# Moving the norm-weight products and the sums of the early banks in the last pass of a GeGLU down projection

## The chip, the cores and the metric

The kernel runs on one core of a Trainium2 chip. A core has five engines with queues of their own: TensorE (PE in the profile, with its weight loads as PEld), VectorE (DVE), ScalarE (ACT), GpSimd (POOL) and SyncE (SP, which here issues nearly all DMA transfers). Each engine works through its queue in order; an instruction that waits for a semaphore holds up everything behind it. The metric is the device time of one execution in microseconds, as the median of three runs.

## The reference, cut to what matters

One decoder layer over 256 tokens of 2048 numbers, in float32. The change touches only its last lines:

```
u = causal_dwconv(h @ w_up[l], conv_w[l], conv_b[l])
gate, val = jnp.split(u, 2, axis=-1)
y = (jax.nn.gelu(gate, approximate=True) * val) @ w_down[l]     # 256 x 5632 @ 5632 x 2048
x = x + rmsnorm(y, post_ffn_g[l])     # y * rsqrt(mean(y*y) + eps) * post_ffn_g
```

A token's row of y must be complete before its reciprocal root (rsqrt of the mean square over all 2048 columns) is known. The product of y with `post_ffn_g` needs no such row and can be made earlier.

## The kernel before, in words

Tokens are in two tiles of 128 (t = 0, 1), the 2048 output columns in four blocks of 512 (n = 0 to 3). The down projection runs in two halves of the 5632 inner rows, and each half in two passes over the columns, n = 0 with 1 and n = 2 with 3. So there are four passes, and the last is half 1, columns 1024 to 2047. Each pass reads 22 blocks of 128 rows of `w_down`, in 11 units of two blocks, each block 128x1024 (512 KB).

A float32 product is made of three passes of a faster format (`product`, line 964): high times high, high times low and low times high. For that each weight block is split: ScalarE copies it rounded (`split`, line 312, the high part `whi`), and VectorE subtracts that from the original (line 313, the low part `wlo`). A low part of 128x1024 is one VectorE instruction. TensorE cannot do the second of three matmuls before it.

Four units of a pass (`FAST`) go by a scheme of seven products in place of eight, with sums of weight quarters (lines 1007 to 1013, VectorE) and of activations. Their first four products gather in the early banks m1, m5, m7, m6 (PSUM tag acc), the others in the late banks p2, p3, p4, p22 (tag att), where the other units gather too. After the last `FAST` unit `add_early` adds the early banks to y in SBUF: one ScalarE copy of m1 into `s`, and eight VectorE sums of 128x512. In the last pass, `HOLD` = 3 units are held back: their parts are made and kept, and `block(i)` runs their 18 matmuls for one late bank after the other, so that one block of y is complete while the next still runs. This is the kept part. The last of the three units has its parts in a tile `rest`. Block 3 is made in two pieces of 256 columns.

`down(t, n, ...)` (line 1087) completes a block of y: VectorE adds the bank (line 1090), ScalarE squares with a row sum (line 1091), GpSimd multiplies by the norm's weights `gbf` (line 1092, called "the product" below). It runs for columns n = 0 and 1 at the end of the third pass, and for n = 2 and 3 in the kept part. `before_last` and `rstd_y` (lines 1160 to 1172) make the reciprocal root: two small VectorE instructions, after the last square one more (line 1169), then a GpSimd power (line 1171). `finish` (line 1175) is one VectorE instruction per block, y times the root plus the residual `x_back`, and the store of the block.

Before the kept part a planner sets the order of each engine but TensorE, whose order is the written one. In the kept part the written order holds for all of them.

Of the kernel before, what the change touches and what calls it, by code (L numbers as in the profile page):

```python
# [12 lines left out]
ALU = mybir.AluOpType  # L13
# [18 lines left out]
def hybrid_layer(ctx: ExitStack, tc: tile.TileContext, x, pre_mix_g, w_in, b_forget, sinks,  # L32
# [814 lines left out]
    with tc.tile_pool(name="ffn", bufs=1) as fp:  # L847
# [122 lines left out]
        def fast_pass(G, sums, order, k00, c0, load, tb, early, late, add_early, hold=1,  # L970
                      keep=None):

            left, right = slice(0, 512), slice(512, UNIT)
            fast = [u for u in order if u in FAST]

            def of(k, t):
                return G[k][:, t * P:(t + 1) * P], G[k][:, 256 + t * P:256 + (t + 1) * P]

            def parts(src, n, into=None):
                hi, lo = into or w_parts(n)  # L980
                split(hi, lo, src)
# [12 lines left out]
            for u in order:  # L994
                k = 2 * u
                ra, rb = (load(w_rows(w_down, k00 + k + a, 1, c0, UNIT)) for a in range(2))
                if u in FAST:
                    i = FAST.index(u)
                    end = u == fast[-1]

                    def s_of(j):
                        return (sums[:, i, j * P:(j + 1) * P],
                                sums[:, i, 512 + j * P:512 + (j + 1) * P])

                    b11 = parts(ra[:, left], 512)
# [12 lines left out]
                    product(m5, *s_of(0), f13, left, first(m5), end)  # L1018
                    product(m7, *s_of(2), f13, right, first(m7), end)
                    product(m6, *s_of(1), f24, left, first(m6), end)  # L1020
                    product(p4, *of(k + 1, 1), f24, right, first(p4), False)
                    product(p2, *of(k + 1, 0), b2, left, first(p2), False)
                    product(p3, *s_of(3), b2, right, first(p3), False)
                    if end:
                        add_early()
                    continue
                b = [parts(r, UNIT, keep[a] if keep and u == order[-1] else None)
                     for a, r in enumerate((ra, rb))]
                if u in order[-hold:]:
                    held += [(k + a, b[a]) for a in range(2)]  # L1030
                    continue
                for a in range(2):
                    for bk, t, cols in blocks:
                        product(bk, *of(k + a, t), b[a], cols, first(bk),
                                hold > 1 and bk is p22 and u == order[-hold - 1] and a == 1)

            def block(i, bk=None, cols=None):
                b, t, c = blocks[i]
                for n, (k, w) in enumerate(held):
                    product(bk or b, *of(k, t), w, cols or c, bk is not None and n == 0,  # L1040
                            n == len(held) - 1, cols and slice(cols.start - 512, cols.stop - 512))

            return block
# [3 lines left out]
        for half in range(2):  # L1047
# [31 lines left out]
                        sums = main.tile([P, len(FAST), UNIT], F32R, tag="x", name="sums")  # L1079
                    token_sums(sums[:, FAST.index(g), :], *ys)  # L1080
            if half == 1:
                late_room = main.tile([P, 4 * D], F32, tag="hT", name="late_room")
                gbf = late_room[:, 0:D]
                x_back = late_room[:, D:3 * D].rearrange("p (t c) -> p t c", t=2)
                sp.dma_start(gbf, post_ffn_g[0].partition_broadcast(P))

            def down(t, n, b, h=None, into=None):
                i, cs = (n, slice(0, 512)) if h is None else (n + h, slice(h * 256, h * 256 + 256))
                ys = y_sb[:, t, n * 512:(n + 1) * 512][:, cs]
                dve.tensor_tensor(ys, b[:, cs], ys, op=ALU.add)  # L1090
                act.activation(junk[:, cs], ys, AF.Square, accum_out=ysq[t][:, i:i + 1])
                pool.tensor_tensor(ys if into is None else into, ys,
                                   gbf[:, n * 512:(n + 1) * 512][:, cs], op=ALU.mult)

            extra = fp.tile([P, 2, UNIT], F32, tag="gbc", name="extra")
            tb = fp.tile([P, 3, UNIT], F32, tag="room", name="tb")
# [11 lines left out]
            for n in (0, 2):  # L1108
                early, late = ([bank(tag) for _ in range(4)] for tag in ("acc", "att"))
                order = list(range(FHALF // 2))  # L1110
                if n == 0:
                    order[:9] = [1, 3, 0, 5, 2, 7, 4, 8, 6]
                elif half:
                    for t in range(2):
                        sp.dma_start(x_back[:, t, :], x_dram[t * P:(t + 1) * P, :])

                def y_of(t, c):
                    return y_sb[:, t, (n + c) * 512:(n + c + 1) * 512]
# [54 lines left out]

        def finish(t, cs, r, q, y=None):
            dve.scalar_tensor_tensor(y_sb[:, t, cs], y_sb[:, t, cs] if y is None else y, r,
                                     x_back[:, t, cs], op0=ALU.mult, op1=ALU.add)
            q.dma_start(of[t * P:(t + 1) * P, cs], y_sb[:, t, cs])

        ctx.enter_context(tc.manual_schedule(
            engines={mybir.EngineType.Activation, mybir.EngineType.DVE, mybir.EngineType.Pool,  # L1180
                     mybir.EngineType.SP}))
        block(0)
        down(0, 2, late[0])
        v = before_last(0, 3)
        block(1)
        down(0, 3, late[1])
        r = rstd_y(0, 3, v)
        for n in range(4):
            finish(0, slice(n * 512, (n + 1) * 512), r, sp)
        block(2)  # L1190
        down(1, 2, late[2])
        last = fp.tile([P, 256], F32, tag="last", name="last")
        for h in range(2):
            if h:
                v = before_last(1, 4)
            b = bank()
            block(3, b, slice(512 + h * 256, 768 + h * 256))
            down(1, 3, b, h, last if h else None)
        r = rstd_y(1, 4, v)
        for i, n in enumerate((512, 512, 512, 256, 256)):  # L1200
            c = (0, 512, 1024, 1536, 1792)[i]
            finish(1, slice(c, c + n), r, (sp, act)[i % 2], last if i == 4 else None)
# [29 lines left out]
```

## Time and profile before

| | |
|---|---|
| median of 3 runs | 1070.96 us (1070.40 to 1071.10) |
| the profiled execution's own time | 1070.95 us |
| its span, first to last instruction | 1069.2 us |
| TensorE busy | 1052.4 us (98%), granted clock 0.997 |
| VectorE, ScalarE, GpSimd busy | 843.4, 637.2, 224.8 us |
| third pass of `down` ends, last pass starts | about 998 us |
| kept part starts, TensorE's last matmul ends | about 1042 us, 1060.2 us |

Times in what follows are microseconds from the span's start. In a timeline a row gives the start, the length, the engine, the line, the operation, the tiles, the count of equal instructions that follow each other, and in brackets the idle time before it with what ended it. Instructions of one engine overlap a little: the next one starts some 0.08 us before the former ends.

### The profile page before, as it was taken

How to read it: one execution, taken by the hardware profiler on the slowest of the kernel's cores; microseconds unless marked ns; L12 is line 12 of the kernel's file. 1: busy time of each engine (PE TensorE's matmuls, PEld its weight loads, DVE VectorE, ACT ScalarE, POOL GpSimd, SP SyncE). 2: the span in 40 equal slices, each digit the busy share in tenths (PEclk: the TensorE clock that was granted, in tenths of full speed). 3: DMA queues.
4: the chain of work that ended last, by engine and by line, in shares of the span. 5: the costliest groups of instructions: out<-in, count | busy, mean ns of one | idle time of the engine just before them, and what ended most of it. 6: DMA issues, size and time to landing. Idle time of an engine off the chain costs nothing.

```text
span 1069.2 us, 16290 instructions
## 1 busy us (share of the span) xinstructions
PE 1052.4 (98%) x5890; PEld 912.9 (85%) x5890; DVE 843.4 (79%) x1369; ACT 637.2 (60%) x1096; POOL 224.8 (21%) x256
## 2 busy tenths in 40 slices
PE   9999999999999999999999999999999999999996
PEld 7889988887889988888888888888888888888785
DVE  5988877887567887787767989668777787788995
ACT  7766766666556765565655556446555565656561
POOL 3233343342022121221212000002121211200202
PEclk9999999999999999999999999999999999999998
DMA  8645657555873776665666566666566666685552
GB/s 291 206 120 174 180 160 210 161 153 156 300 248 106 266 229 188 192 190 181 211 186 191 192 203 209 215 187 197 167 209 190 190 191 195 192 301 191 167 175 79
DMA packets 154284, 207.08 MB, mean 194 GB/s; under 512 B 6844, under 2 KB 131036, under 8 KB 153180
## 3 DMA queue, kind: packets, MB, share of 16 engines
q1 hardware_dynamic: 153200, 203.37, 60.5%
q10 hardware_dynamic: 1004, 2.68, 0.6%
q8 instruction: 46, 0.75, 0.3%
q14 instruction: 34, 0.28, 0.1%
HBM read 201.68 MB, written 4.21 MB: 193 GB/s over the span
## 4 chain that ended last, share of the span: by engine, by line
PE 90%; DVE 4%; DMA 2%; issue 2%; POOL 1%; ACT 1%; SPq 0%; DVEq 0%; POOLq 0%; ACTq 0%
PE bank_acc L284 16%; PE bank_att L967 14%; PE bank_att L284 14%; PE bank_acc L309 12%; PE bank_acc L290 8%; PE bank_att L290 7%; PE bank_acc L253 6%; PE bank_acc L967 4%; PE bank_acc L258 3%; PE bank_att L475 1%; DVE wlo L313 1%; PE bank_att L510 1%; DVE wlo L115 1%; PE bank_acc L932 1%; DMA x_in<-in_x_dram 1%
## 5 line engine op out<-in xcount | busy, mean ns | idle before, releaser
L115 DVE TENSOR_TENSOR wlo<-raw,whi 128x1024 fp32r<-128x1024 f32 (+3 forms) x271 | 330.1, 1228 | 117.1 <-ACT whi L112 112.4
L112 ACT CAST whi<-raw 128x1024 fp32r<-128x1024 f32 (+3 forms) x270 | 273.3, 1029 | 124.4 <-issue 88.9
L899 POOL TENSOR_TENSOR room<-room,rowf 128x256 f32<-128x256 f32 x88 | 100.3, 1160 | 393.9 <-DVE room L898 392.1
L284 PE MATMUL bank_acc<-hT,whi 128*128 128x512 f32 x736 | 173.3, 390 | 0.0
L284 PEld LDWEIGHTS bank_acc<-hT,whi 128*128 128x128 f32 x736 | 136.5, 188 | 27.3
L967 PE MATMUL bank_att<-whi,G 128*128 128x512 f32 x488 | 156.2, 389 | 0.0
L284 PE MATMUL bank_att<-hT,whi 128*128 128x512 f32 x640 | 150.6, 390 | 0.0
L284 PEld LDWEIGHTS bank_att<-hT,whi 128*128 128x128 f32 x640 | 118.7, 188 | 23.8
L967 PEld LDWEIGHTS bank_att<-whi,G 128*128 128x128 f32 x488 | 91.6, 188 | 18.9
L967 PE MATMUL bank_att<-wlo,G 128*128 128x512 f32 x244 | 95.2, 390 | 2.4 <-DVE wlo L313 2.4
L290 PEld LDWEIGHTS bank_acc<-hT,wlo 128*128 128x128 f32 x736 | 89.3, 188 | 2.0
L290 PE MATMUL bank_acc<-hT,wlo 128*128 128x256 f32 x736 | 89.9, 279 | 0.0
L253 PE MATMUL bank_acc<-hT,whi 128*128 128x512 f32 x352 | 89.2, 396 | 0.0
L901 ACT ACTIVATE room<-room,cw 128x256 f32<-128x256 f32 x88 | 53.0, 602 | 60.6 <-POOL room L899 60.6
L309 PE MATMUL bank_acc<-whi,oT 128*128 128x512 f32 (+1 forms) x272 | 82.5, 380 | 0.0
L290 PEld LDWEIGHTS bank_att<-hT,wlo 128*128 128x128 f32 x640 | 77.6, 188 | 1.7
L290 PE MATMUL bank_att<-hT,wlo 128*128 128x256 f32 x640 | 77.9, 279 | 0.0
L903 DVE SCALAR_TENSOR_TENSOR room<-room,cw 128x256 f32<-128x256 f32 x88 | 62.4, 709 | 17.5 <-ACT room L901 17.3
L313 DVE TENSOR_TENSOR wlo<-raw,whi 128x1024 fp32r<-128x1024 f32 (+1 forms) x56 | 62.4, 1138 | 13.4 <-ACT whi L312 13.4
L253 PEld LDWEIGHTS bank_acc<-hT,whi 128*128 128x128 f32 x352 | 63.0, 188 | 11.3
L312 ACT CAST whi<-tb 128x1024 fp32r<-128x1024 f32 x42 | 44.0, 1050 | 45.0 <-PE bank_att L967 19.2
L312 ACT CAST whi<-raw 128x1024 fp32r<-128x1024 f32 (+1 forms) x56 | 52.4, 958 | 28.8 <-PE bank_att L967 22.2
(254 smaller groups left out, 1589.9 us busy)
## 6 DMA issues: line engine op xcount, KB each, us to landing
raw<-in_w_up_dram SPq DMA_DIRECT2D x176, 512.0 KB, 4.1
raw<-in_w_down_dram SPq DMA_DIRECT2D x58, 512.0 KB, 4.8
raw<-in_w_in_dram SPq DMA_DIRECT2D x51, 512.0 KB, 3.9
raw<-in_w_out_dram SPq DMA_DIRECT2D x32, 512.0 KB, 4.7
extra<-in_w_down_dram SPq DMA_DIRECT2D x20, 512.0 KB, 3.8
raw<-in_w_in_dram SPq DMA_DIRECT2D x16, 384.0 KB, 3.4
tb<-in_w_down_dram SPq DMA_DIRECT2D x10, 512.0 KB, 4.8
cb<-c_dram SPq DMA_DIRECT2D x8, 256.0 KB, 3.6
```

Source lines behind the costliest of these rows:

```text
L112: i1 = act.copy(hi[:, cs], raw[:, cs])
L115: i2 = dve.tensor_tensor(lo[:, cs], raw[:, cs], hi[:, cs].bitcast(F32), op=ALU.subtract)
L253: pe.matmul(b, parts[u][0][:, a, m * P:(m + 1) * P], hT[:, kt, :], start=(kt == 0), stop=(kt == KT - 1))
L284: pe.matmul(b, parts[u][0][:, a, m * P:(m + 1) * P], hT[:, kt, :], start=(kt == 0), stop=(kt == KT - 1))
L290: pe.matmul(b[:, 256:512], parts[u][1][:, a, m * P:(m + 1) * P], hT[:, kt, 0:256], start=False, stop=False)
L309: pe.matmul(b, a, r[:, cols], start=(first and i == 0), stop=(last and i == 2))
L312: act.copy(hi, src)
L313: dve.tensor_tensor(lo, src, hi.bitcast(F32), op=ALU.subtract)
L899: pool.tensor_tensor(u[:, 2:258], u[:, 2:258], rowf, op=ALU.mult)
L901: act.activation(y, u[:, 2:258], AF.Identity, bias=cw[:, 3, ch:ch + 1], scale=cw[:, 2, ch:ch + 1])
L903: dve.scalar_tensor_tensor(y, u[:, 1:257], cw[:, 1, ch:ch + 1], y, op0=ALU.mult, op1=ALU.add)
L967: pe.matmul(b[:, to] if to else b, a, r[:, cols], start=(first and i == 0), stop=(last and i == 2))
```

## The change

1. `down` makes no product any more. The products of all blocks are made by a new function `gain`, called in the kept part.
2. In the last pass `add_early` is called after the loop over the units (`if hold > 1`), no longer inside it. In the other passes it stays.
3. The residual `x_back` is no longer loaded into its own room at the third pass's start, but into two buffers, `tb[:, 0:2]` and `extra`, that served as room for sums and weights, at the start of the kept part as written.
4. Two of the four `finish` of token tile 0 come after the sum of block (1, 2).
5. In the tail the power for token tile 1 comes ahead of the last product.

```
-                    if end:
+                    if end and hold == 1:
                         add_early()
...
+            if hold > 1:
+                add_early()
...
-                late_room = main.tile([P, 4 * D], F32, tag="hT", name="late_room")
-                gbf = late_room[:, 0:D]
-                x_back = late_room[:, D:3 * D].rearrange("p (t c) -> p t c", t=2)
+                gbf = main.tile([P, 4 * D], F32, tag="hT", name="gbc_ffn")[:, 0:D]
...
+            def gain(t, n, h=None, into=None):
+                cs = slice(0, 512) if h is None else slice(h * 256, h * 256 + 256)
+                ys = y_sb[:, t, n * 512:(n + 1) * 512][:, cs]
+                pool.tensor_tensor(ys if into is None else into, ys,
+                                   gbf[:, n * 512:(n + 1) * 512][:, cs], op=ALU.mult)
...
-                pool.tensor_tensor(ys if into is None else into, ys,
-                                   gbf[:, n * 512:(n + 1) * 512][:, cs], op=ALU.mult)
...
-                elif half:
-                    for t in range(2):
-                        sp.dma_start(x_back[:, t, :], x_dram[t * P:(t + 1) * P, :])
...
+        x_back = [tb[:, 0:2, :].rearrange("p a c -> p (a c)"),
+                  extra.rearrange("p a c -> p (a c)")]
+        for t in range(2):
+            sp.dma_start(x_back[t], x_dram[t * P:(t + 1) * P, :])
+        gain(0, 0)
+        gain(0, 1)
         block(0)
         down(0, 2, late[0])
+        gain(0, 2)
+        gain(1, 0)
         v = before_last(0, 3)
         block(1)
         down(0, 3, late[1])
         r = rstd_y(0, 3, v)
-        for n in range(4):
+        gain(0, 3)
+        gain(1, 1)
+        for n in range(2):
             finish(0, slice(n * 512, (n + 1) * 512), r, sp)
         block(2)
         down(1, 2, late[2])
+        gain(1, 2)
+        for n in range(2, 4):
+            finish(0, slice(n * 512, (n + 1) * 512), r, sp)
...
-            down(1, 3, b, h, last if h else None)
+            down(1, 3, b, h)
+            if h == 0:
+                gain(1, 3, 0)
         r = rstd_y(1, 4, v)
+        gain(1, 3, 1, last)
```

GpSimd, all that it has to do after the up projection. Before, the eight products stand in the order of `down` (0,0), (0,1), (1,0), (1,1), (0,2), (0,3), and behind the first power (`ry`) (1,2) and the two halves of (1,3):

```order
L1092 TENSOR_TENSOR y_sb<-y_sb,late_room 128x512 x6
L1171 TENSOR_TENSOR ry<-rv,mhalf 128x1
L1092 TENSOR_TENSOR y_sb<-y_sb,late_room 128x512
L1092 TENSOR_TENSOR y_sb<-y_sb,late_room 128x256
L1092 TENSOR_TENSOR last<-y_sb,late_room 128x256
L1171 TENSOR_TENSOR ry<-rv,mhalf 128x1
```

Changed, the first four are (0,0), (0,1), (0,2), (1,0), and the three behind the first power (0,3), (1,1), (1,2):

```order
L1091 TENSOR_TENSOR y_sb<-y_sb,gbc_ffn 128x512 x4
L1173 TENSOR_TENSOR ry<-rv,mhalf 128x1
L1091 TENSOR_TENSOR y_sb<-y_sb,gbc_ffn 128x512 x3
L1091 TENSOR_TENSOR y_sb<-y_sb,gbc_ffn 128x256
L1173 TENSOR_TENSOR ry<-rv,mhalf 128x1
L1091 TENSOR_TENSOR last<-y_sb,gbc_ffn 128x256
```

The products (0,0) and (0,1) are still the first in GpSimd's queue behind the up projection's work, and each waits for the square of its own block alone; (1,0) and (1,1) now stand behind instructions that wait for blocks of the kept part; the second power stands ahead of the last product.

VectorE in the last pass, from the low part of the unit behind the last `FAST` one (before; `s` and `y_sb` in the outputs are `add_early`, `wlo` and `rest` low parts):

```order
L1131 TENSOR_TENSOR y_sb<-s,y_sb 128x512
L313 TENSOR_TENSOR wlo<-extra,whi 128x1024
L1132 TENSOR_TENSOR s<-bank_acc,s 128x512
L313 TENSOR_TENSOR wlo<-extra,whi 128x1024
L1133 TENSOR_TENSOR y_sb<-s,y_sb 128x512
L313 TENSOR_TENSOR wlo<-tb,whi 128x1024
L1134 TENSOR_TENSOR y_sb<-bank_acc,y_sb 128x512
L1135 TENSOR_TENSOR s<-bank_acc,s 128x512
L313 TENSOR_TENSOR wlo<-raw,whi 128x1024
...
L313 TENSOR_TENSOR rest<-raw,rest 128x1024
L1138 TENSOR_TENSOR y_sb<-s,y_sb 128x512
L313 TENSOR_TENSOR rest<-raw,rest 128x1024
```

Changed:

```order
L313 TENSOR_TENSOR wlo<-extra,whi 128x1024
L1133 TENSOR_TENSOR y_sb<-s,y_sb 128x512
L313 TENSOR_TENSOR wlo<-extra,whi 128x1024
L313 TENSOR_TENSOR wlo<-tb,whi 128x1024
L313 TENSOR_TENSOR wlo<-raw,whi 128x1024
L313 TENSOR_TENSOR rest<-raw,rest 128x1024 x2
L313 TENSOR_TENSOR wlo<-raw,whi 128x1024
L1134 TENSOR_TENSOR s<-bank_acc,s 128x512
L1135 TENSOR_TENSOR y_sb<-s,y_sb 128x512
L1136 TENSOR_TENSOR y_sb<-bank_acc,y_sb 128x512
```

One sum is left ahead of the last low part; seven stand behind it.

SyncE at the end of the last pass (changed):

```order
L1110 DMA tb<-in_w_down_dram 128x1024
L69 DMA raw<-in_w_down_dram 128x1024 x3
L1187 DMA tb<-x_dram 128x2048
L69 DMA raw<-in_w_down_dram 128x1024
L1187 DMA extra<-x_dram 128x2048
L1179 DMA out_dram<-y_sb 128x512 x6
```

The first residual load stands ahead of the pass's last weight load; it waits until VectorE has read `tb` for the last time as room for sums.

More of the change, by code (lines that the diff above doesn't have):

```diff
@@ L1081, in hybrid_layer, with down @@
             if half == 1:
-                late_room = main.tile([P, 4 * D], F32, tag="hT", name="late_room")
-                gbf = late_room[:, 0:D]
-                x_back = late_room[:, D:3 * D].rearrange("p (t c) -> p t c", t=2)
+                gbf = main.tile([P, 4 * D], F32, tag="hT", name="gbc_ffn")[:, 0:D]
                 sp.dma_start(gbf, post_ffn_g[0].partition_broadcast(P))
-            def down(t, n, b, h=None, into=None):
+            def gain(t, n, h=None, into=None):
[3 more added lines that the diff above has]
+                                   gbf[:, n * 512:(n + 1) * 512][:, cs], op=ALU.mult)
+            def down(t, n, b, h=None):
                 i, cs = (n, slice(0, 512)) if h is None else (n + h, slice(h * 256, h * 256 + 256))
@@ L1175, in finish @@
             dve.scalar_tensor_tensor(y_sb[:, t, cs], y_sb[:, t, cs] if y is None else y, r,
-                                     x_back[:, t, cs], op0=ALU.mult, op1=ALU.add)
+                                     x_back[t][:, cs], op0=ALU.mult, op1=ALU.add)
             q.dma_start(of[t * P:(t + 1) * P, cs], y_sb[:, t, cs])
```

## The prediction

> **What bounds the kernel now.** First the waits of TensorE, over the whole span:
>
> ```profile
> PE bank_att L967 <- DVE wlo L313: 2.4, 2, 1.8
> PE bank_att L967 <- DVE rest L313: 1.1, 2, 0.8
> ```
>
> The page gives TensorE 98% of the span busy. A change at the end can therefore win only where TensorE still waits, and behind its last matmul. The two rows (us, times, longest) are the two places in the last pass: the handoff from the third pass, and the start of the kept part. Both wait for low parts, that is for VectorE. TensorE's timeline gives what each costs:
>
> ```profile
> 1001.04 0.61 PE L967 MATMUL bank_att<-whi,G 128*128 128x512 f32 x2
> 1003.44 0.50 PE L967 MATMUL bank_att<-wlo,G 128*128 128x512 f32 x1 [1.79 <-DVE wlo L313]
> ...
> 1004.71 0.40 PE L967 MATMUL bank_att<-whi,G 128*128 128x512 f32 x1
> 1005.67 0.50 PE L967 MATMUL bank_att<-wlo,G 128*128 128x512 f32 x1 [0.57 <-DVE wlo L313]
> ...
> 1012.82 0.61 PE L967 MATMUL bank_acc<-whi,sums 128*128 128x512 f32 x2
> 1013.35 0.50 PE L967 MATMUL bank_acc<-wlo,sums 128*128 128x512 f32 x1
> ...
> 1044.54 0.39 PE L967 MATMUL bank_att<-rest,G 128*128 128x512 f32 x1
> ...
> 1047.55 0.39 PE L967 MATMUL bank_att<-whi,G 128*128 128x512 f32 x1
> ...
> 1050.28 1.52 PE L967 MATMUL bank_att<-rest,G 128*128 128x512 f32 x6
> ```
>
> Undisturbed, six matmuls take 1.52 with 0.39 for the last, so one starts every 0.226. The first matmul behind a wait lasts 0.50 in place of 0.39, so a wait costs 0.11 beyond its idle time. The six `rest` matmuls of block 0 should take 6 x 0.226 = 1.36 and take 1047.55 - 1044.54 = 3.01: 1.65 are lost there.
>
> Why VectorE is late at the handoff shows when GpSimd's rows stand beside its own, and the undisturbed low part last:
>
> ```profile
> 997.09 1.29 POOL L1092 TENSOR_TENSOR y_sb<-y_sb,late_room 128x512 f32<-128x512 f32 x1 [53.40 <-ACT junk L1091]
> 1000.96 1.34 POOL L1092 TENSOR_TENSOR y_sb<-y_sb,late_room 128x512 f32<-128x512 f32 x1 [0.34 <-ACT junk L1091]
> 1002.66 1.88 POOL L1092 TENSOR_TENSOR y_sb<-y_sb,late_room 128x512 f32<-128x512 f32 x1 [0.35 <-ACT junk L1091]
> ```
>
> ```profile
> 997.38 2.09 DVE L313 TENSOR_TENSOR wlo<-tb,whi 128x1024 fp32r<-128x1024 f32 x1
> ...
> 1001.69 1.70 DVE L313 TENSOR_TENSOR wlo<-tb,whi 128x1024 fp32r<-128x1024 f32 x1
> 1003.31 2.31 DVE L313 TENSOR_TENSOR wlo<-raw,whi 128x1024 fp32r<-128x1024 f32 x1
> ```
>
> ```profile
> L313 DVE TENSOR_TENSOR wlo<-extra,whi 128x1024 fp32r<-128x1024 f32 x3 | 3.6, 1217 | 0.0
> ```
>
> A low part takes 1.22 alone. The one at 997.38 meets the product that ends at 998.38, and ends 1.09 after it; the one at 1001.69 ends 1.09 after the third product's end at 1002.30; the one at 1003.31 ends 1.08 after the fourth's at 1004.54. So while a product runs, a VectorE instruction with both inputs in SBUF stands still and then runs nearly whole. Who is next when both want it shows in the up phase:
>
> ```profile
> 710.44 2.31 POOL L899 TENSOR_TENSOR room<-room,rowf 128x256 f32<-128x256 f32 x2 [30.94 <-DVE room L898]
> ```
>
> ```profile
> 710.92 1.24 DVE L115 TENSOR_TENSOR wlo<-raw,whi 128x1024 fp32r<-128x1024 f32 x1 [0.23 <-ACT whi L112]
> 712.09 0.95 DVE L903 SCALAR_TENSOR_TENSOR room<-room,cw 128x256 f32<-128x256 f32 x1
> ```
>
> GpSimd's second product waits for the low part (710.92 + 1.24 = 712.16), goes next, ends at 710.44 + 2.31 = 712.75, and holds up the instruction that VectorE starts at 712.09. They take turns.
>
> **The handoff.** The change's words suggest that all four products leave this place. Two do. The products (0,0) and (0,1) are still first in GpSimd's queue and wait only for their squares, so they run at 997.09 as before, and the 2.09 stays. The third and fourth in the queue are now (0,2) and (1,0), which stand still until the kept part. That frees the other two low parts: 1.70 - 1.22 = 0.48 and 2.31 - 1.22 = 1.09, together 1.57 of VectorE. TensorE's first wait then ends at 1003.44 - 0.48 = 1002.96. Undisturbed it would want the next low part at 1004.71 + 0.23 - 0.48 = 1004.46; that part ended at 1005.62 and now ends 1.57 earlier, at 1004.05. No second wait: 1005.67 - 1004.46 = 1.21, and 0.11 for the slow first matmul. A third, small stop goes too: the matmul at 1013.35 came 0.08 late (1012.82 + 2 x 0.226 = 1013.27) and cost 0.11 more, and its low part comes 1.57 sooner while TensorE comes 1.32 sooner. The handoff gives 1.32 + 0.19 = **1.51**.
>
> **The kept part.** Here VectorE's rows are
>
> ```profile
> 1032.95 1.23 DVE L313 TENSOR_TENSOR wlo<-raw,whi 128x1024 fp32r<-128x1024 f32 x1 [1.50 <-ACT whi L312]
> 1034.09 0.69 DVE L1131 TENSOR_TENSOR y_sb<-s,y_sb 128x512 f32<-128x512 f32 x1
> ```
>
> and then, in turn, seven low parts and seven more sums up to TensorE's second wait. Now eight low parts and one sum come first: 8 x 1.22 + 0.69 = 10.45 at most, from 1032.95 - 1.51 = 1031.44 to 1041.9. The last of them is the second weight block of the middle held unit, wanted by the eleventh matmul of block 0. Block 0 starts 12 matmuls ahead of 1044.54, at 1041.83, now 1040.32, so it is wanted at 1042.58. There are 0.7 to spare, and all of the **1.65** comes back. The seven sums then run while TensorE is in blocks 0 and 1; 7 x 0.69 = 4.8, some ahead of and some behind `down` (0,2), all over before the bank of block 1 is full. With the handoff TensorE is ahead by 1.51 + 1.65 = **3.16**.
>
> **The tail.** It does not keep all of that. Before:
>
> ```profile
> 1051.84 0.69 DVE L1090 TENSOR_TENSOR y_sb<-bank_att,y_sb 128x512 f32<-128x512 f32 x1 [2.27 <-PE bank_att L967]
> 1053.38 0.16 DVE L1169 SCALAR_TENSOR_TENSOR rv<-ysq,rv 128x1 f32<-128x1 f32 x1 [0.85 <-ACT junk L1091]
> 1055.25 2.74 DVE L1175 SCALAR_TENSOR_TENSOR y_sb<-y_sb,ry,late_room 128x512 f32<-128x512 f32 x4 [1.71 <-POOL ry L1171]
> ...
> 1059.98 0.16 DVE L1162 TENSOR_REDUCE st_y<-ysq 128x1 f32<-128x4 f32 x1 [1.06 <-ACT junk L1091]
> ...
> 1060.25 0.42 DVE L1090 TENSOR_TENSOR y_sb<-bank_acc,y_sb 128x256 f32<-128x256 f32 x1
> 1061.24 0.22 DVE L1169 SCALAR_TENSOR_TENSOR rv<-ysq,rv 128x1 f32<-128x1 f32 x1 [0.57 <-ACT junk L1091]
> 1062.66 2.47 DVE L1175 SCALAR_TENSOR_TENSOR y_sb<-y_sb,ry,late_room 128x512 f32<-128x512 f32 x4 [1.21 <-POOL ry L1171]
> ```
>
> ```profile
> 1061.40 0.72 POOL L1092 TENSOR_TENSOR last<-y_sb,late_room 128x256 f32<-128x256 f32 x1
> 1062.09 0.54 POOL L1171 TENSOR_TENSOR ry<-rv,mhalf 128x1 f32<-128x1 f32 x1
> ```
>
> Changed: the sum of (0,3) starts at 1051.84 - 3.16 = 1048.68, the small `rv` ends at 1050.38, the power (0.54, nothing ahead of it now) at 1050.97. Behind the power stand the moved products (0,3) and (1,1), on VectorE the first two `finish`, both inputs in SBUF, and they take turns: a product to 1052.24 (1.29 alone), a `finish` of 0.67 (2.74 for four) to 1052.9, a product to 1054.2, a `finish` to 1054.87. So two products hold up VectorE by 2.6 here. The sum of (1,2), which reads PSUM, 0.6; two `finish` to 1056.8 (the product (1,2) waits for its square meanwhile); then the sum of the first half of (1,3). Before, the next `rv` came 0.99 after such a sum's start (1060.25 to 1061.24), so the reduction starts at 1057.72 and the last sum 0.27 behind it, at 1057.99. TensorE is ready 3.16 before 1060.25, at 1057.09: 0.9 are given back, and this point is 2.26 ahead. The next `rv` then ends at 1059.20, and the power starts there and not behind `last`: 1062.09 - 2.26 - 1059.23 = 0.60 won. But `last` now runs while `finish` wants to, from 1059.74 to 1060.46, and `finish` goes on from there instead of from 1062.66: 2.20 ahead. The reordered power is worth nothing, since `last` still stands in the way of the same instruction.
>
> The Trainium skill (SBUF — State Buffer, "Who interferes with whom") says that VectorE with two SBUF inputs and a GpSimd instruction that reads SBUF exclude each other for a whole instruction, and whichever issues first holds the pair. The trace agrees: the low part at 1003.31 loses 1.09 of the 1.23 for which the product still runs. Were the interface shared in halves instead, the tail would lose 1.3 and not 2.6, and half of `last`, and the sum would come to about 1067.5.
>
> The rest I cost at nothing. The residual loads leave a place where TensorE did not wait. ScalarE's copies change their order a little; if they came late, they would first use up the 0.7 spare, and then cost TensorE what they are late. The products (0,2) and (1,0) and, behind them, the first power wait in GpSimd's queue; the square of (0,2) comes near 1046, so both are over by 1049, ahead of the power at 1050.4. **Sum:** 1070.95 - 2.20 = 1068.75, in span 1067.0; the profiled execution stands at the runs' median (1070.96), so 1068.7 is my number.
>
> **Rivals.** *The turns cost less.* POOL spans are rough, and the turn rule rests on one place. With no conflict in the tail, the last sum waits for TensorE alone: 3.16 + 0.60 = 3.76, 1067.2; with `last` alone in conflict, 1067.9. For it: that nothing here shows a `finish` against a product; against it: line 903, the same kind of instruction, doubles from 0.48 to 0.95. *One product more gets in.* If (1,2) comes ahead of the fourth `finish`, another 1.2 goes: 1069.9. By my times its square ends some 0.3 after that `finish` starts, a thin margin. *All four products leave the handoff.* Then the 2.09 becomes 1.22 and the first wait shrinks by 0.87 more: with the tail's loss 1067.9. Against it stands GpSimd's order. *The weight load behind the residual.* The slower side:
>
> ```profile
> 1027.79 2.50 DVE L313 TENSOR_TENSOR wlo<-tb,whi 128x1024 fp32r<-128x1024 f32 x2
> ```
>
> ```profile
> DMA to landing us min/median/max: 8.0/8.9/9.9
> ```
>
> ```profile
> 1031.48 0.33 SPq L69 DMA_DIRECT2D raw<-in_w_down_dram  x1
> ```
>
> The 1 MB residual load goes out when the low parts of `tb` are done, 1030.29 - 1.5 = 1028.8, ahead of the last 512 KB of weights. Two copies of 1.0 and a low part of 1.22 lie between that landing and 1042.58, so from 1039.3 on each us late costs one. If it lands only after a whole residual load as slow as the two before (9.9, to 1038.7) and half of such a load's median again, 1043.2: 3.9 late, 1072.6. With little else in the queues I expect it near 1037. The Trainium skill (DMA: Bandwidth & Descriptors, "Queues, rings and completion order") has descriptors of one ring consumed in order, which makes the load wait its turn but shares all engines; no run here shows this order yet.
>
> **The numbers.** My forecast 0.50 (own range 1068.1 to 1069.3), turns cheaper 0.20, one product more 0.21, all four leave 0.05, late weight load 0.04. A measurement of this kernel tells about 0.2%, 2.1 us, from no change: 1068.8 is the line, just above my number. Faster by that: half of the first, all of the second and fourth, 0.53; slower by it needs more than even the last rival gives, 0.03; the rest, 0.44, within. The range 1067.2 to 1069.9 leaves out the late load and the edges.
>
> **What would show it.** Two products still at 997 and none at 1001 to 1004; one TensorE wait left in the handoff, about 1.3; none at `rest`; TensorE's last matmul near 1057.0; the first `finish` of token tile 0 stretched to about 2 us, and the first of tile 1 to 1.4; the last sum behind VectorE's own queue and not behind TensorE. I am wrong if TensorE waits in the kept part, if the `finish` rows keep 0.74 beside running products, or if the last weight load lands after 1039.

## The result, and the profile after

| | before | changed |
|---|---|---|
| median (13 runs of each, side by side) | 1071.47 us (1070.33 to 1073.34) | 1068.31 us (1067.23 to 1070.82) |
| ratio | | 0.9971, 95% interval 0.9963 to 0.9979 |
| a second comparison (18 and 6 runs) | 1071.67 us | 1067.95 us, ratio 0.9968 (0.9955 to 0.9980) |

The changed kernel is faster by 0.3%. Two of its executions were profiled. I call them A (1067.23 us, span 1065.5, the quickest of its 13) and B (1067.99 us, span 1066.3, close to the median). Both are needed, because A shows more than the change: its gain over the profiled execution of before is 3.7 us, and B's 2.9.

What TensorE still waits for in the last pass (the waits view; us in total, times, longest), first in A, then in B:

```profile
PE bank_att L967 <- DVE wlo L313: 0.4, 1, 0.4
```

```profile
PE bank_att L967 <- DVE wlo L313: 1.1, 1, 1.1
```

Of the four waits before, one is left, and none is for `rest`. TensorE's timeline, first its last six matmuls before, then A and B:

```profile
1059.31 0.88 PE L967 MATMUL bank_acc<-rest,G 128*128 128x256 f32 x6
```

```profile
1002.00 0.50 PE L967 MATMUL bank_att<-wlo,G 128*128 128x512 f32 x1 [0.36 <-DVE wlo L313]
...
1042.05 1.52 PE L967 MATMUL bank_att<-rest,G 128*128 128x512 f32 x6
1043.41 0.39 PE L967 MATMUL bank_att<-whi,G 128*128 128x512 f32 x1
...
1055.16 0.88 PE L967 MATMUL bank_acc<-rest,G 128*128 128x256 f32 x6
```

```profile
1002.81 0.50 PE L967 MATMUL bank_att<-wlo,G 128*128 128x512 f32 x1 [1.10 <-DVE wlo L313]
...
1042.86 1.52 PE L967 MATMUL bank_att<-rest,G 128*128 128x512 f32 x6
...
1055.97 0.88 PE L967 MATMUL bank_acc<-rest,G 128*128 128x256 f32 x6
```

The six `rest` matmuls now take their 1.36 (1042.05 to 1043.41). The last six of the pass (the very last starts 0.60 later) start at 1055.16 and 1055.97, against 1059.31 before. A and B run the same instructions, yet the remaining wait is 0.4 in one and 1.1 in the other. The chain of waits names the difference; A, then B:

```profile
974.55 4.81 DMA extra<-in_w_down_dram
1002.00 6.87 PE bank_att L967 x29
```

```profile
974.62 5.55 DMA extra<-in_w_down_dram
1002.81 6.87 PE bank_att L967 x29
```

One weight load of the third pass, issued at the same time, took 4.81 in A and 5.55 in B. VectorE waits for it and is then busy without a gap until the handoff. The rows for before, A and B, in this order:

```profile
980.41 0.69 DVE L1007 TENSOR_TENSOR tb<-extra 128x512 f32<-128x512 f32 x1 [2.43 <-DMA extra<-in_w_down_dram]
```

```profile
979.45 0.69 DVE L1007 TENSOR_TENSOR tb<-extra 128x512 f32<-128x512 f32 x1 [1.49 <-DMA extra<-in_w_down_dram]
...
996.42 2.08 DVE L313 TENSOR_TENSOR wlo<-tb,whi 128x1024 fp32r<-128x1024 f32 x1
```

```profile
980.26 0.69 DVE L1007 TENSOR_TENSOR tb<-extra 128x512 f32<-128x512 f32 x1 [2.23 <-DMA extra<-in_w_down_dram]
...
997.22 2.10 DVE L313 TENSOR_TENSOR wlo<-tb,whi 128x1024 fp32r<-128x1024 f32 x1
999.84 1.18 DVE L1007 TENSOR_TENSOR tb<-raw 128x512 f32<-128x512 f32 x1
1001.54 1.21 DVE L313 TENSOR_TENSOR wlo<-tb,whi 128x1024 fp32r<-128x1024 f32 x1
1002.67 1.21 DVE L313 TENSOR_TENSOR wlo<-raw,whi 128x1024 fp32r<-128x1024 f32 x1
...
1048.50 0.69 DVE L1097 TENSOR_TENSOR y_sb<-bank_att,y_sb 128x512 f32<-128x512 f32 x1 [1.28 <-PE bank_att L967]
1050.86 3.48 DVE L1177 SCALAR_TENSOR_TENSOR y_sb<-y_sb,ry,tb 128x512 f32<-128x512 f32 x2 [0.66 <-POOL ry L1173]
1054.26 0.68 DVE L1097 TENSOR_TENSOR y_sb<-bank_att,y_sb 128x512 f32<-128x512 f32 x1
1054.86 1.40 DVE L1177 SCALAR_TENSOR_TENSOR y_sb<-y_sb,ry,tb 128x512 f32<-128x512 f32 x2
...
1057.49 0.42 DVE L1097 TENSOR_TENSOR y_sb<-bank_acc,y_sb 128x256 f32<-128x256 f32 x1
1059.31 2.92 DVE L1177 SCALAR_TENSOR_TENSOR y_sb<-y_sb,ry,extra 128x512 f32<-128x512 f32 x4 [0.66 <-POOL ry L1173]
```

From that sum to the long low part it is 16.97 in before (980.41 to 997.38), 16.97 in A and 16.96 in B. So A came 0.96 earlier to the handoff than before did, for a reason that is no part of the change. B came 0.15 earlier, and is the one to hold against before.

GpSimd in B:

```profile
996.94 3.53 POOL L1091 TENSOR_TENSOR y_sb<-y_sb,gbc_ffn 128x512 f32<-128x512 f32 x2 [53.20 <-ACT junk L1098]
1045.94 2.89 POOL L1091 TENSOR_TENSOR y_sb<-y_sb,gbc_ffn 128x512 f32<-128x512 f32 x2 [45.47 <-ACT junk L1098]
1050.28 0.55 POOL L1173 TENSOR_TENSOR ry<-rv,mhalf 128x1 f32<-128x1 f32 x1 [1.45 <-DVE rv L1171]
1050.79 3.00 POOL L1091 TENSOR_TENSOR y_sb<-y_sb,gbc_ffn 128x512 f32<-128x512 f32 x2
1055.83 2.25 POOL L1091 TENSOR_TENSOR y_sb<-y_sb,gbc_ffn 128x512 f32<-128x512 f32 x2 [2.04 <-ACT junk L1098]
1058.72 0.55 POOL L1173 TENSOR_TENSOR ry<-rv,mhalf 128x1 f32<-128x1 f32 x1 [0.64 <-DVE rv L1171]
1059.24 0.72 POOL L1091 TENSOR_TENSOR last<-y_sb,gbc_ffn 128x256 f32<-128x256 f32 x1
```

Two products at 997 and none at 1001 to 1004; the products (0,3) and (1,1) at 1050.79 beside the first two `finish`, which take 3.48 for two in place of 1.40; and the first `finish` of tile 1 beside `last` (2.92 for four in place of 2.47).

The place where VectorE starts that sum after the load gives a fixed point, and the span splits in four. The parts are differences between rows: that start; from it to the first `rest` matmul; from there to the last six matmuls; from there to the end of the span. The profiled executions of this case but one, those of the experiments below among them (the span is known to 0.1 us, so the part "to the end" is good to 0.05):

| kernel | sum starts | to `rest` | to the last six | to the end | span |
|---|---|---|---|---|---|
| before | 980.41 | 64.13 | 14.77 | 9.89 | 1069.2 |
| changed, A | 979.45 | 62.60 | 13.11 | 10.34 | 1065.5 |
| changed, B | 980.26 | 62.60 | 13.11 | 10.33 | 1066.3 |
| sums only | 980.94 | 64.17 | 13.11 | 9.88 | 1068.1 |
| all but the sums | 982.33 | 62.59 | 14.78 | 10.30 | 1070.0 |
| residual loads back | 980.43 | 62.58 | 13.11 | 10.28 | 1066.4 |
| two added products | 982.44 | 62.59 | 13.11 | 10.36 | 1068.5 |
| two products left out | 981.84 | 62.60 | 13.11 | 9.75 | 1067.3 |
| `last` ahead of the power | 981.24 | 62.66 | 13.12 | 9.98 | 1067.0 |
| all four leave | 980.17 | 61.29 | 13.12 | 10.32 | 1064.9 |
| all four leave, (1,1) ahead ("both moves") | 979.87 | 61.88 | 13.12 | 9.73 | 1064.6 |
| the same, `last` ahead | 980.05 | 61.54 | 13.11 | 9.40 | 1064.1 |

With an equal start the change wins 1.53 in the handoff and 1.66 in the kept part and gives 0.45 back in the tail: **2.74** (0.26%, inside both intervals). The prediction's sum was 1.51, 1.65 and 0.96 given back: 2.20. The medians differ by 3.16; no row here assigns the 0.4 between that and 2.74.

In the last three rows the second column measures nothing fixed: no matmul waits for VectorE at the handoff any more, TensorE's own pace sets the first `rest` matmul, and the sum's start no longer does.

### The profile page after: what moved, and what is told of

Its sections match the earlier page's. It is cut to its first block, busy times and chain, and to the rows that moved or that the text cites. A ratio compares the mean times of both kernels' runs of the same rounds, so it can differ in the third digit from the quotient of the medians.

```text
span 1065.5 us, 16294 instructions
## 1 busy us (share of the span) xinstructions
PE 1051.2 (99%) x5890; PEld 913.3 (86%) x5890; DVE 843.8 (79%) x1369; ACT 637.6 (60%) x1096; POOL 225.9 (21%) x256
## 3 DMA queue, kind: packets, MB, share of 16 engines
q10 hardware_dynamic: 1004, 2.68, 0.6%
## 4 chain that ended last, share of the span: by engine, by line
PE 91%; DVE 4%; DMA 1%; POOL 1%; issue 1%; ACT 1%; SPq 0%; DVEq 0%; POOLq 0%; ACTq 0%
PE bank_acc L284 16%; PE bank_att L967 15%; PE bank_att L284 14%; PE bank_acc L309 12%; PE bank_acc L290 8%; PE bank_att L290 7%; PE bank_acc L253 7%; PE bank_acc L258 3%; PE bank_acc L967 3%; PE bank_att L475 1%; PE bank_att L510 1%; DVE wlo L115 1%; DVE wlo L313 1%; PE bank_acc L932 1%; DMA x_in<-in_x_dram 1%
```

## Experiments

**The two halves of the change.** First the sums alone:

```
-                    if end:
+                    if end and hold == 1:
                         add_early()
...
+            if hold > 1:
+                add_early()
```

> The kernel before, with one edit: in the last pass the sums of the early banks come behind the loop over the units. Products, residual loads, finish and tail stay. Theory (two separate waits of TensorE, each with its own cause): the handoff keeps its waits on the low parts, 1.8 and 0.6 us (2.4 in all, up to 1 us less if a weight load lands early), four products run there; no wait at rest (1.1 before). TensorE ends 1.65 us sooner and the tail, unchanged, follows it: 1.65 us less, ratio 0.9985. Rival (the sums are only pushed behind and hold up the sums of blocks 0 and 1): nothing won, ratio 1.000, and the sum of block (0,3) starts later than TensorE's end of block 1.

Measured: ratio 0.9982 (0.9973 to 0.9990). TensorE's waits in the last pass:

```profile
PE bank_att L967 <- DVE wlo L313: 1.6, 2, 1.1
```

Then everything but the sums: the changed kernel with

```
-                    if end and hold == 1:
+                    if end:
                         add_early()
...
-            if hold > 1:
-                add_early()
```

> The changed kernel with that one edit undone: the sums of the early banks stay among the low parts. Theory: handoff as in the changed kernel (two products, one TensorE wait of 0.4 to 1.3 us), the wait at rest of 1.1 back; the tail gives back about 0.6 of the 1.5 by two finish of 1.8 us, and wins 0.1 from the reordered power. 1.0 to 1.1 us less than before, ratio 0.9990; with the other edit alone this adds to the whole, 2.7. Rival (the edits help only together): ratio 1.000 here.

Measured: ratio 0.9984 (0.9975 to 0.9993), and both waits for `rest` are back (the longest wait at the handoff is 1.8, more than expected, at a sum that starts 2.1 later than in B):

```profile
PE bank_att L967 <- DVE wlo L313: 1.9, 2, 1.8
PE bank_att L967 <- DVE rest L313: 1.1, 2, 0.8
```

The table shows the two halves better than the ratios do. The sums change only the third column (14.77 to 13.11), and all the rest changes only the second and the fourth (64.13 to 62.59, 9.89 to 10.30). The kept part's term is separate from the handoff's and has the predicted size. The two reductions, 0.18% and 0.16%, add up to that of the whole within their intervals.

**The handoff and the load ahead of it.** The changed kernel once more, unaltered; its profiled execution is B:

> The changed kernel once more, as a control on this chip and for a second profiled execution. Ratio 0.9971. By my reading of the handoff its first wait for a low part goes with the landing of the weight load that VectorE waits for at about 980: landed at 979.4 it is 0.4; each us of later landing adds up to one us there, until TensorE's other waits set the pace. If that landing is as in the kernel before (980.3), the wait is about 1.3 and the span 1066.4; if the landing has nothing to do with it, the wait is 0.4 again wherever the load lands.

The start was within 0.15 of that of before, and the wait is 1.10, where the prediction had about 1.3; 0.15 of the difference is the earlier start. The landing theory holds: wait and start moved together, and the span is 1066.3. To make VectorE late by an instruction and not by chance, two products of 128x256 were added on GpSimd in the third pass, on a tile that VectorE has just written:

```
+                    if end and hold == 1 and k00:
+                        scr = fp.tile([P, 256], F32, tag="last", name="scr")
+                        for _ in range(2):
+                            pool.tensor_tensor(scr, t13[:, 0:256], t13[:, 256:512], op=ALU.mult)
```

> The changed kernel with two more products of 128x256 on GpSimd near 983, into a tile that nobody reads until later, in turns with VectorE there: an instruction of work that changes no order on VectorE and makes it about 1.0 us later at the handoff (two meetings of 0.3 to 0.7). Theory: VectorE has no idle time from the weight load that it waits for at 980 to the handoff, so TensorE's first wait there grows by as much: with a landing as before about 1.1 + 1.0 = 2.1, the kept part's start 1.0 later, ratio 0.9980. Rival, that other waits of VectorE on the way or slack of TensorE take it up: wait 1.1 for a landing at 980.3, ratio 0.9971.

Measured: ratio 0.9984 (0.9975 to 0.9993), so 1.5 us above the first median of the changed kernel, where 1.0 was expected. GpSimd's timeline and VectorE's:

```profile
970.73 2.80 POOL L1019 TENSOR_TENSOR scr<-tb 128x256 f32<-128x256 f32 x2 [25.61 <-DVE tb L1007]
```

```profile
971.71 1.23 DVE L1008 TENSOR_TENSOR tb<-raw 128x512 f32<-128x512 f32 x1
972.86 1.22 DVE L1011 TENSOR_TENSOR tb<-raw,tb 128x512 f32<-128x512 f32 x1
...
982.44 0.69 DVE L1007 TENSOR_TENSOR tb<-extra 128x512 f32<-128x512 f32 x1 [2.61 <-DMA extra<-in_w_down_dram]
```

I had the place wrong: the products ran at 971, ahead of the load, not at 983 behind it. Two sums that take 0.69 alone took 1.23 and 1.22, so VectorE lost 1.07 there. It freed the load's buffer later, the sum after the load started at 982.44, and the first `rest` matmul came 62.59 behind it, as in A and B. Lateness ahead of that sum is passed on whole; the rival, that slack takes it up, is out in the rows. TensorE's wait was 1.80 and not the expected 2.1, since TensorE too came later to that matmul, at 1003.18 against 1001.71 in B. Not all of the 2.2 between this execution and B is from the products: VectorE was 1.4 later already where they begin (the sum that starts at 968.57 in B starts at 969.96 here). What makes executions of one kernel differ there was not tried.

The residual loads back in a room of their own, issued in the third pass (942.10 and 948.91) as in the kernel before:

```
-        x_back = [tb[:, 0:2, :].rearrange("p a c -> p (a c)"),
-                  extra.rearrange("p a c -> p (a c)")]
-        for t in range(2):
-            sp.dma_start(x_back[t], x_dram[t * P:(t + 1) * P, :])
+        x_back = [xb[:, 0, :], xb[:, 1, :]]
```

> The changed kernel with the residual loaded at the third pass's start into a room of its own, as before, so that the last weight load has no residual load ahead of it. My theory: ScalarE's idle 0.7 us ahead of the last cast of weights goes, TensorE does not wait in the kept part either way, and the time is that of the changed kernel: ratio 0.9971, within 0.0005. Rival, that the residual loads late in the pass cost (the last low part comes close to TensorE's need of it): 0.3 to 0.7 less, 0.9965 to 0.9968. Second rival, that loads early in the pass take bandwidth from the weight loads at the handoff: later by as much, 0.9976.

Measured: ratio 0.9973 (0.9960 to 0.9986), and behind the start no part of the table differs from B by more than 0.05. In A, ScalarE did wait 0.72 for the last weight load, which stands behind a residual load:

```profile
1036.81 1.05 ACT L312 CAST rest<-raw 128x1024 fp32r<-128x1024 f32 x1 [0.72 <-DMA raw<-in_w_down_dram]
```

The landing near 1036.8 is about the predicted one (near 1037), and TensorE did not wait. In B, the same kernel, that cast starts at once, as it does in this run, so it isn't shown that this edit takes the idle 0.72 away. By the rows, moving the residual loads neither costs nor wins.

**All four products out of the handoff.** A GpSimd instruction that waits for the last `FAST` unit's sums stands ahead of the first product:

```
+        gate_col = small.tile([P, 1], F32, tag="st", name="gate_col")
+        pool.tensor_copy(gate_col, tb[:, 1, 1023:1024])
...
         gain(0, 0)
         gain(0, 1)
```

> The changed kernel, and ahead of GpSimd's first product a copy of one number that VectorE writes with the last of its sums of weights in the last pass (its result is not used). So no product runs in the handoff; (0,0) and (0,1) run from about 1025, where VectorE has 1.5 us of idle time ahead of the kept part's low parts. Theory (what is left of the handoff wait is the two products that did not leave): the low part after the third pass takes 1.22 and not 2.08, no TensorE wait on a low part is left there, 0.6 to 1.4 us less than the changed kernel: ratio 0.9960. Rival (the wait left there is a late weight load's): TensorE still waits 0.4 or more at the handoff, ratio 0.997. Rival (the two products only carry their price to another place): a TensorE wait of up to 1 us between 1026 and 1042.

Measured: ratio 0.9959 (0.9946 to 0.9972). No wait of TensorE is left in the last pass. GpSimd's timeline, then VectorE's:

```profile
1024.74 1.12 POOL L1187 COPY gate_col<-tb 128x1 f32<-128x1 f32 x1 [81.00 <-DVE tb L1013]
1025.82 3.53 POOL L1091 TENSOR_TENSOR y_sb<-y_sb,gbc_ffn 128x512 f32<-128x512 f32 x2
```

```profile
997.14 1.22 DVE L313 TENSOR_TENSOR wlo<-tb,whi 128x1024 fp32r<-128x1024 f32 x1
...
998.87 0.68 DVE L1007 TENSOR_TENSOR tb<-raw 128x512 f32<-128x512 f32 x1
...
1024.60 3.60 DVE L313 TENSOR_TENSOR wlo<-tb,whi 128x1024 fp32r<-128x1024 f32 x2
```

A and B had shown that two products stay by themselves; this prices it. B's wait of 1.10, with 0.11 for the slow first matmul, is gone, and TensorE sets its own pace; the table has 1.31 (62.60 to 61.29), and 0.72 and 1.06 in the two later rows that also lack these products, so 1.31 is this execution's figure. The prediction gave 0.87 for it. It had counted one of two meetings, the first product's with the long low part (2.10 against 1.22), and not the second product's with a sum (1.18 in B at 999.84, 0.68 here). The products do carry their price to another place: two low parts that take 2.50 in B take 3.60 here at 1024.60. But VectorE has idle time there (1.49 ahead of the low part at 1031.27 in B), and no wait of TensorE comes of it.

**One meeting less in the tail.** The product (1,1) directly behind (1,0), ahead of the power:

```
         gain(0, 2)
         gain(1, 0)
+        gain(1, 1)
...
         gain(0, 3)
-        gain(1, 1)
```

> The changed kernel with product (1,1) moved ahead of the first power, behind (1,0). Theory (GpSimd and VectorE take turns, about 1.05 us for each product that meets a finish): GpSimd is done with it by 1049.4, just ahead of the power; one finish of 1.8 us and three of 0.74 are left for token tile 0; the last sum comes at TensorE's pace, 0.6 us sooner than in the changed kernel, ratio 0.9966 or 0.9965. Rival (the tail has room for both products): the last sum stands as it did against TensorE, no change from the changed kernel, 0.9971. If the power waits for the product instead, the first finish starts later and nothing is won either.

Measured: ratio 0.9968 (0.9958 to 0.9978), which does not tell the two theories apart. Its profiled execution isn't in the table, since TensorE ran slower there for 3 us behind the handoff (a matmul every 0.43 in place of 0.227). The tail is undisturbed, and it does tell them apart: from the last six matmuls (1059.17) to the end of the span (1068.9) it is 9.73, 0.6 less than in B, as the first theory has it:

```profile
1054.06 2.44 DVE L1177 SCALAR_TENSOR_TENSOR y_sb<-y_sb,ry,tb 128x512 f32<-128x512 f32 x2 [0.66 <-POOL ry L1173]
...
1060.08 0.42 DVE L1097 TENSOR_TENSOR y_sb<-bank_acc,y_sb 128x256 f32<-128x256 f32 x1 [0.35 <-PE bank_acc L967]
```

Two `finish` take 2.44 in place of 3.48, so one meeting costs 1.04, and the last sum waits for TensorE again. The two moves together:

> The changed kernel with both moves of the two runs before: no product left in the handoff, and the product (1,1) directly behind (1,0), so that only (0,3) meets a finish of tile 0. My theory: the handoff gain as with all four gone, TensorE without a wait in the last pass, one finish stretched to about 1.8 and three at 0.74, so one meeting of 1.04 less; the last sum then follows TensorE. In all 0.3 to 0.6 below the run with all four gone: ratio to before 0.9956, about 1067.0 us. Rival (the tail has slack, and the meetings cost nothing once the last sum waits for something else): 0.9960, as with all four gone.

Measured: ratio 0.9950 (0.9937 to 0.9963), median 1066.08. That is 1.4 below the median with all four gone, where 0.3 to 0.6 was expected; the spans of the two profiled executions differ by 0.3. The tail is 9.73 against 10.32, so 0.59 come back for one meeting less, though a meeting takes 1.04: once one is gone, TensorE ends the wait and not VectorE.

**No meeting in the tail,** the term that was most wrong, by itself:

```
-        gain(0, 3)
-        gain(1, 1)
         for n in range(2):
             finish(0, slice(n * 512, (n + 1) * 512), r, sp)
```

> The changed kernel without the products (0,3) and (1,1): these two blocks of the output lack the norm's weights. It takes the two meetings of product and finish in the tail away. Theory: the first two finish take 0.74 each, VectorE is through earlier, and the last sum waits for TensorE: it starts 0.3 after the start of TensorE's last matmul (0.34 in the kernel before, 0.92 in the changed kernel), so 0.56 to 0.6 are won, ratio 0.9965. The prediction's size of the tail's loss: 0.9 won, 0.9963. Rival, that meetings cost nothing at the end because something else holds the last sum: 0.9971 and a last sum still 0.9 behind the last matmul's start.

Measured: ratio 0.9970 (0.9959 to 0.9981), no difference from the changed kernel that the medians show; the start varies by more (981.84 in the profiled execution, 980.26 in B). In the rows the term stands alone:

```profile
1052.44 1.41 DVE L1177 SCALAR_TENSOR_TENSOR y_sb<-y_sb,ry,tb 128x512 f32<-128x512 f32 x2 [0.66 <-POOL ry L1173]
...
1058.47 0.42 DVE L1097 TENSOR_TENSOR y_sb<-bank_acc,y_sb 128x256 f32<-128x256 f32 x1 [0.75 <-PE bank_acc L967]
```

The last sum starts 0.92 behind the last six matmuls' start (1057.55), in B 1.52 (1055.97 to 1057.49), and the tail is 0.58 shorter. Against the changed kernel the two meetings hold up the end by 0.6, not by 0.9.

**`last` and the second power.** The old order of the two, in the changed kernel:

```
-        r = rstd_y(1, 4, v)
         gain(1, 3, 1, last)
+        r = rstd_y(1, 4, v)
```

> The changed kernel with the old order of the last product and the second power: last first. My theory: the power is 0.60 later, but the first finish of tile 1 takes 0.74 in place of 1.20, so the end comes 0.15 later than in the changed kernel, ratio 0.9972. The prediction's sizes (0.60 won, 0.69 lost) have it 0.09 earlier. No median can tell these apart; the rows of the last power and of the four finish of tile 1 can: start of the power behind last at the last square plus about 1.2, first finish 0.74. Rival, that last does not disturb finish at all: 0.60 later, ratio 0.9977.

Measured: ratio 0.9967 (0.9955 to 0.9978). GpSimd's timeline, then VectorE's:

```profile
1059.10 0.72 POOL L1091 TENSOR_TENSOR last<-y_sb,gbc_ffn 128x256 f32<-128x256 f32 x1
1059.91 0.55 POOL L1173 TENSOR_TENSOR ry<-rv,mhalf 128x1 f32<-128x1 f32 x1
```

```profile
1058.54 0.42 DVE L1097 TENSOR_TENSOR y_sb<-bank_acc,y_sb 128x256 f32<-128x256 f32 x1
...
1060.49 2.47 DVE L1177 SCALAR_TENSOR_TENSOR y_sb<-y_sb,ry,extra 128x512 f32<-128x512 f32 x4 [0.66 <-POOL ry L1173]
```

My expectation failed, and its rival too. The power starts 1.37 behind the last sum, against 1.23 in B: the old order makes it later by 0.14, not by 0.60. `last` needs the sum and not its square, and it is over when the power's input is ready. The four `finish` keep 2.47, and the tail is shorter by 0.35. So the fifth edit of the change, the power ahead of `last`, **loses** 0.35.

The 0.60 by which the power comes earlier behind the last sum than before (1.84 then, 1.23 in B) has another source. Before, GpSimd's rows were

```profile
1059.49 1.96 POOL L1092 TENSOR_TENSOR y_sb<-y_sb,late_room 128x512 f32<-128x512 f32 x2 [4.27 <-ACT junk L1091]
```

since the sum of (1,2) stood behind four `finish`, and the products (1,2) and the first half of (1,3) came late and pushed `last`. Counted from the start of TensorE's last six matmuls, these products end at 2.14 before (1059.49 + 1.96 - 1059.31) and still at 2.11 in B (1055.83 + 2.25 - 1055.97), and the power starts at 2.78 and 2.75. So against TensorE the power is no earlier in the changed kernel: the last sum is later, by 0.58. With the turns gone GpSimd is through sooner. With the two products left out, its rows are

```profile
1055.75 2.41 POOL L1091 TENSOR_TENSOR y_sb<-y_sb,gbc_ffn 128x512 f32<-128x512 f32 x2 [3.34 <-ACT junk L1098]
1059.71 0.55 POOL L1173 TENSOR_TENSOR ry<-rv,mhalf 128x1 f32<-128x1 f32 x1 [1.55 <-DVE rv L1171]
```

and the products end at 0.61, the power starts at 2.16 (last six from 1057.55). That the fourth edit, two `finish` behind the sum of (1,2), makes this room is read from the order of the rows; no run has that edit alone.

The old order on top of both moves:

> The run with both moves, and the product last again ahead of the second power. Theory, from the run with the old order alone: there the power came only 0.14 later behind the last sum's start than in the changed kernel, since last waits for the sum alone and not for the square, and each finish kept 0.74, so the last finish came 0.32 earlier behind that sum. The same here: last sum to last finish 4.35 in place of 4.67, so 0.3 less than the run with both moves, ratio 0.9947, about 1065.8 us. Rival, by the prediction's sizes (the power 0.60 later, last costing 0.69): 0.09 less. Second rival, my expectation of the run before (0.60 later, 0.46 won): 0.14 more, ratio 0.9951.

Measured: ratio 0.9946 (0.9934 to 0.9958), median 1065.81. The tail is 9.40, 0.33 less than with both moves alone. Its median is the lowest of this case, and its interval lies below that of the changed kernel's first comparison; from the run with both moves the medians don't tell it apart, only the rows do.

## Why the prediction was right, and where it was not

The median, 1068.31, is 0.4 below the predicted 1068.7, which was made from a before of 1070.96 that measured 1071.47 beside it. Part of this nearness is luck: before came out 0.5 slower, which hides half of what the forecast gain fell short. The gain is the better test: 2.20 predicted (ratio 0.9979, the upper end of the interval), 3.16 by the medians, 2.74 by the rows at an equal start. What fell short is the tail, in which the prediction gave back 0.96 and the rows 0.45.

- **The handoff, 1.51.** Right in kind and size: 1.53. Two products left and two stayed; the first wait ended at 1002.81 in B, with VectorE 0.15 earlier than before, against 1002.96 predicted; the second wait is gone.
- **The kept part, 1.65.** Right: 1.66, in the run with the sums alone too. No low part was late.
- **The tail, 0.9 given back at the last sum.** Right in kind, too large. The turns of (0,3) and (1,1) with the first two `finish` were there, and the last sum stood behind VectorE's queue. The step that failed is the price of a turn, a full product of 1.29 plus the `finish`. A `finish` beside a product took 1.78 against 0.74, so it cost 1.04, and both 2.1 and not 2.6. The rows show how: the first `finish` ends at 1052.6, 0.55 after the product's end (1050.79 + 1.29 = 1052.08), though it takes 0.74 alone. The prediction's own rows had shown this: the low part at 1003.31 lost 1.09 of the 1.23 for which the product still ran. In the other direction, the reduction came 1.05 behind the start of its sum (1056.18 to 1057.23) where 0.92 was counted. Together they leave 0.58 at the last sum.
- **`last` against the first `finish` of tile 1, 0.69.** Right in kind; it measured 0.45 (2.92 against 2.47), the same error.
- **The power, 0.60 won.** The size held only as counted from the last sum (1.84 before, 1.23 now), and the cause did not: the order of power and `last` makes 0.14 of it, and the rest is the last sum's own lateness, since from TensorE's last six matmuls the power starts at 2.78 before and 2.75 in B. So the tail's 0.45 is about what `last` costs the `finish`. That the reorder is worth nothing was too kind; it costs 0.35.
- **What was costed at nothing** held for the residual loads. What was missed is that VectorE's time at the handoff hangs on a load 17 us earlier, which lands up to 1 us apart at equal issue. The prediction took before's profiled execution for a fixed point. In A this was worth 0.96 of the 3.7.

The Trainium skill (SBUF — State Buffer, "Who interferes with whom") has VectorE and GpSimd exclude each other for a whole instruction. The runs agree that they take turns, but the loser lost 1.04 beside an instruction of 1.29, and 0.45 beside one of 0.72, each begun only 0.07 earlier. By these rows a part of one runs beside the other; the profile's GpSimd spans are rough, so this isn't settled.

Of the rivals, *all four leave* did not happen by itself and, made to happen, measured 0.9959. *One product more* did not: (1,2) started at 1055.83, while the fourth `finish` was running, and the two `finish` kept 1.40. *The late weight load* did not. *The turns cost less* was right in part: by a fifth for a product, by a third for `last`. (The chances that the prediction names for a time below 1068.8 add up to 0.50, not to its 0.53.)

## What to carry to other kernels

Before costing a change at a wait, find the last point upstream where the waiting engine itself waited for a transfer, and measure from there: here 62.6 us behind one sum the profiled executions that kept the two products in the handoff agreed within 0.1 (but for the one in which TensorE ran slower), while two executions of one kernel differed by 0.8 with the landing of one load. Work on GpSimd that meets VectorE took most of its length from the waiting chain here (1.04 of 1.29), so put it where the profile shows VectorE with spare; moving two products by one gating instruction took away TensorE's last wait of the pass, 1.10. A distance between two rows shrinks also when the earlier one comes late: measure a gain from an engine that the edit leaves alone, and time the edits of one change apart.

## What was not expected of the hardware

- A 512 KB load with the same issue time (974.55 and 974.62) took 4.81 and 5.55 to land, and the difference arrived at the end of the kernel whole. What makes it vary stays open.
- A one-element-per-row copy on GpSimd took 1.12 (1024.74) where the power of one element per row takes 0.55.
- Two products and two `finish` that start together go strictly in turns: 3.00 and 3.48 in B, where they would take 2.5 and 1.40 apart, so both engines lose.
